# Rotary tables made first: positions with the constants, steps between the row tiles' scalings, sines stored ahead of the second half's norm

## The chip, the core and the metric

The kernel runs on one core of a Trainium2 chip. The metric is the device time of one execution in microseconds (us), as the median of several runs. TensorE (PE) does the matmuls, VectorE (DVE), ScalarE (ACT) and GpSimd (POOL) the elementwise work; SyncE (SP) issues nearly all DMAs. Each engine works through its own instructions in a fixed order and waits on semaphores.

## The reference

Two decoder layers on x of 1024 tokens by 1024, float32. The first layer mixes tokens by sliding-window attention with rotary embedding of the first quarter of each head (64 wide), the second by a gated recurrence; each is set between two RMS norms and added to x.

```python
def partial_rope(x, positions):          # half = 8 of 64
    inv_freq = ROPE_THETA ** (-(arange(8) * 2.0 / 16))
    ang = positions[..., None] * inv_freq
    cos, sin = cos(ang), sin(ang)        # per token and frequency
    r1 = x1 * cos - x2 * sin
    r2 = x2 * cos + x1 * sin
...
h = rmsnorm(x, pre_norm_w[0])
q, k, v, z = split(h @ w_in + b_in)
q, k = partial_rope(q), partial_rope(k)
o = softmax over a window of 128 keys (q k^T / 8, with a sink per head) @ v
x = x + rmsnorm((o * silu(z)) @ w_out + b_out, post_norm_w[0])
... (second layer: projections, chunked recurrence, projection)
```

## The kernel before

Matmuls are done in three products of split operands: a weight tile `wraw` (128 x 512, 256 KB) is loaded by SP, split into a rounded high part `whi` (POOL for the first 20 tiles, ACT later) and a remainder `wlo` (DVE; POOL for tiles 2 and 3). Four `wraw` buffers rotate, so tile i+4 is loaded only when tile i has been split. Activations are split the same way: a transposed block `pst` in PSUM becomes `acth` (ACT) and `actl` (DVE).

The start: the 1024 rows come in two halves of four row tiles of 128. `x_load(o0, 0)` loads the first half, ACT squares each row tile, POOL makes the inverse root `rstd`, DVE scales the row tile (`norm_rows`), PE transposes it (L237), and the first two projections (values, and a quarter of the queries, `q_unit(0, 1, 0)`) run on the first half of the tokens. The second half, `xh1`, goes the same way after it: four squares (L225), four `rstd`, four scalings, transposes. Then come `q_unit(0, 2, 0)`, `q_unit(0, 3, 0)`, `q_unit(0, 0, 0)` (the one whose result is rotated: `qf`, `qtB`, L355 to L361) and `k_unit` (keys, rotated: `kf`, `tK`, `KH`, `KL`). `kw` are the split weight tiles 10 and 11 of the keys. `vmid`, `VX` belong to the values.

The rotary tables: DVE makes the angles from `pos` in about 25 small steps on 128 x 64 or 128 x 256 elements (tiles `rt`, `a1r`), ACT takes the sines (`cs`, L302 and L307, after a table load), POOL negates one (L308), SP stores them to `csd` in DRAM and reads them back, broadcast to all partitions, as `cosT` (512 KB), two halves of `sinT` (256 KB each), and four small pieces into `cosK`. The DVE steps are issued a few at a time between other work: `at` gives how many at each place (`some()`).

Queries go to DRAM in pieces (`qd`, L367) and come back transposed by head and block as `QS` (L497), which the first attention scores (`pss`, L514) read.

What sets the order: a scheduler orders the instructions of each engine by priority and by its own estimate of times. `tc.high_priority` and `hp()` raise the priority; with `v.on` DVE's instructions keep the order in which they are written; `tc.issue_after` puts an instruction behind another one. PSUM tiles rotate through two buffers per tag (`mm`, `t`, `s`, `o`), so that a transpose or a product also waits until the tile two before it on its tag has been read.

Of the kernel before, what the change touches and what calls it, by code (L numbers as in the profile page):

```python
# [89 lines left out]
def emit(tc, I, out):  # L90
    nc = tc.nc
    v = InOrder(tc, nc.vector)
    from contextlib import ExitStack
    top = ExitStack()
    with top:
# [13 lines left out]
        pos = const.tile([P, 64], I32, name="pos")  # L109
# [8 lines left out]
        def hp():  # L118

            return tc.high_priority(offset=HP)  # L120
# [10 lines left out]
        def fetch(end):  # L131
            while W["fetch"] < min(end, NS):
                f = W["fetch"]
                W["dmas"][f] = nc.sync.dma_start(wraw[f % NR], I["w"][f])
                W["fetch"] += 1

        def advance(end=NS):

            while W["split"] < end:
                i = W["split"]  # L140
                fetch(i + NR)
                if i in (W_K, W_K + 1):
                    W["place"][i] = W["keys"][i - W_K]
                elif W["free"]:
                    W["place"][i] = W["free"].pop(0)
                else:
                    return
                raw, (hi, lo) = wraw[i % NR], W["place"][i]
                with hp():
                    on_pool = i in (2, 3)  # L150
                    if i < 20:
                        nc.gpsimd.tensor_scalar(hi, raw, 1.0, 1.0, op0=ALU.mult, op1=ALU.mult)
                    else:
                        nc.scalar.activation(hi, raw, AF.Copy)  # L154
                    W["split_ins"][i] = (nc.gpsimd if on_pool else v).tensor_tensor(lo, raw, hi.bitcast(F32), op=ALU.subtract)  # L155
                W["split"] += 1
# [20 lines left out]
        def act_from_psum(k, half, ps, scale):  # L177
            hi, lo = act[k, half]
            ins = nc.scalar.activation(hi, ps, AF.Copy, scale=scale)
            W["actl"][k] = v.scalar_tensor_tensor(lo, ps, scale, hi.bitcast(F32), op0=ALU.mult, op1=ALU.subtract)  # L180
            return ins
# [51 lines left out]
        def transpose_half(hns, half, scol, then={}):  # L233
            for k in range(NK):
                pt = pp.tile([P, 512], F32, tag="tso"[k % 3], name="pst")
                for j in range(4):
                    nc.tensor.transpose(pt[:, j * P:(j + 1) * P], hns[j][:, k * P:(k + 1) * P], ident)  # L237
                ins = act_from_psum(k, half, pt, cst[:, scol + k:scol + k + 1])
                then.get(k, lambda: None)()
            return ins  # L240
# [13 lines left out]
        def x_load(xh, half):  # L254
            for j in range(4):
                t = half * 4 + j
                for cs in halves(t):
                    nc.sync.dma_start(xh[:, j, cs], I["x"][t * P:(t + 1) * P, cs])
# [14 lines left out]
        def rope_tables(sp, cosT, sinT, cosK, tK):  # L273

            ang, a2, acc = [sp.tile([P, 64], F32, name=f"rt{i}") for i in range(3)]
            t0, t1 = [sp.tile([P, 4, 64], F32, name=f"rt{i}") for i in (3, 4)]
            a1r = sp.tile([P, 64], F32R, name="a1r")
            a1 = a1r.bitcast(F32)
            c1, c2, c3 = _split12(1.0 / (2.0 * np.pi), 2)

            def neg_frac(x):

                t = t1 if x is t0 else t1[:, 0, :]
                return [lambda: v.tensor_scalar(t, x, MAGIC, None, op0=ALU.add),
                        lambda: v.scalar_tensor_tensor(x, t, MAGIC, x, op0=ALU.subtract, op1=ALU.subtract)]

            steps = [lambda: v.tensor_copy(ang, pos),
                     lambda: v.tensor_scalar(ang, ang, cst[:, C_INV:C_INV + 1], None, op0=ALU.mult),
                     lambda: v.tensor_copy(a1r, ang),
                     lambda: v.tensor_tensor(a2, ang, a1, op=ALU.subtract),  # L290
                     lambda: v.tensor_scalar(acc, ang, c3, None, op0=ALU.mult)]
            steps += [lambda i=i, a=a, c=c: v.tensor_scalar(t0[:, i, :], a, c, None, op0=ALU.mult)
                      for i, (a, c) in enumerate(((a1, c1), (a1, c2), (a2, c1), (a2, c2)))]
            steps += neg_frac(t0) + neg_frac(t0)
            steps += [lambda i=i: v.tensor_tensor(acc, acc, t0[:, i, :], op=ALU.add) for i in range(4)]
            steps += neg_frac(acc)

            def last():
                cs3 = sp.tile([P, 3, 64], F32, name="cs3")
                lim, t2 = 0.49999997, t0[:, 0, :]  # L300
                v.tensor_scalar(t2, acc, lim, -lim, op0=ALU.min, op1=ALU.max)
                nc.scalar.activation(cs3[:, 1, :], t2, AF.Sin, scale=-6.2831853)  # L302
                v.tensor_scalar(acc, acc, -1.0, 0.25, op0=ALU.mult, op1=ALU.add)
                for f in neg_frac(acc):
                    f()
                v.tensor_scalar(t2, acc, lim, -lim, op0=ALU.min, op1=ALU.max)
                nc.scalar.activation(cs3[:, 0, :], t2, AF.Sin, scale=-6.2831853)  # L307
                nc.gpsimd.tensor_scalar(cs3[:, 2, :], cs3[:, 1, :], -1.0, 1.0, op0=ALU.mult, op1=ALU.mult)  # L308

                nc.sync.dma_start(csd.rearrange("i j (c n) -> (j c) i n", n=64), cs3)  # L310
                nc.sync.dma_start(cosT, csd[0:1].to_broadcast([16, 8, T]))
                nc.sync.dma_start(sinT[:64], csd[2:3].to_broadcast([8, 8, T]))
                nc.sync.dma_start(sinT[64:], csd[1:2].to_broadcast([8, 8, T]))
                m32 = sp.tile([P, M_L], I32, name="m32")
                nc.sync.dma_start(m32, I["msk"][:, :M_L])
                with tc.issue_after(W["rstd"].ins):
                    nc.gpsimd.memset(cosK, 1.0)
                    nc.gpsimd.memset(tK, 0.0)
                    nc.gpsimd.tensor_copy(msk, m32)
                for o in range(4):  # L320
                    nc.sync.dma_start(cosK[32 * o:32 * o + 8], csd[0])

            return steps + [last]

        def layer0():
# [3 lines left out]
            cosT = ka.tile([P, T], F32, tag="big0", name="cosT")  # L331
            sinT = ka.tile([P, T], F32, tag="big1", name="sinT")
# [38 lines left out]
            with pool("start", "right") as sp:  # L371
                W["keys"] = [tuple(kw.tile([P, 512], F32R, name=f"kw{i}{l}") for l in range(2)) for i in range(2)]
                kf = kw.tile([P, 512], F32, name="kf")
                tK = kw.tile([P, 512], F32, name="tK")
                cosK = kw.tile([P, T], F32, name="cosK")
                steps = rope_tables(sp, cosT, sinT, cosK, tK)
                at = iter([0, 3, 0, 4, 3, 3, 3])
                some = lambda: [steps.pop(0)() for _ in range(next(at))]
                with tc.high_priority(offset=1000):
                    v.on = True  # L380
                    hn0 = []
                    for j in range(4):
                        if j > 1:
                            some()
                        for cs in halves(j):
                            norm_rows(sp, o0[:, j, cs], o0[:, j, cs], rs0[j])
                        hn0.append(o0[:, j, :])
                    some()
                    advance(1)
                    last = transpose_half(hn0, 0, C_PRE, {2: lambda: advance(4)})  # L390
                xh1 = sp.tile([P, 4, D], F32, name="xh1")
                x_load(xh1, 1)
                hn1 = []
                with tc.high_priority(offset=1000):
                    for j in range(4):
                        with tc.issue_after(last.ins):
                            r = row_rstd(sp, xh1[:, j, :])
                        hn1.append(norm_rows(sp, xh1[:, j, :], xh1[:, j, :], r))
                        some()
                v.on = False  # L400
                with tc.issue_after(W["rstd"].ins):
                    advance()
                with hp():
                    while steps:
                        steps.pop(0)()
                nc.gpsimd.tensor_scalar(hbias, cst[:, C_BIN:C_BIN + 18], 0.5, 1.0, op0=ALU.mult, op1=ALU.mult)

                def k_unit(half):
# [55 lines left out]
            with pool("att", "right") as ap:  # L464
# [113 lines left out]
                at = [3, 5, 7, 7, 9, 11, 14, 14, 17, 19, 20, 23, 25, 27, 27]  # L578
# [362 lines left out]


        nc.scalar.dma_start(cst, I["cst"])
        x_load(o0, 0)
        nc.sync.dma_start(pos, I["pos"].unsqueeze(0).to_broadcast([8, 16, 64]))
        ld = const.tile([P, 9], F32, name="ld")
        v.tensor_tensor(ld[:, :8], cst[:, C_LB:C_LB + 8], cst[:, C_LB + 8:C_LB + 16], op=ALU.subtract)
        v.tensor_reduce(ld[:, 8:], ld[:, :8], axis=AX.X, op=ALU.max)
# [96 lines left out]
```

## Time and profile before

| | |
|---|---|
| runs | 920.67 us median of 3 (918.2 to 920.74) |
| the profiled execution | 919.34 us, span 917.5 us, granted clock 0.995 |
| PE busy | 891.1 us (97%) |
| DVE, ACT, POOL busy | 551.2, 373.7, 342.1 us |
| DMA | 78.61 MB, mean 86 GB/s |

The profile comes from one execution; its times are counted from the first instruction of the span. A view of waits tells which engine sat idle before an instruction, until what; the chain follows the work that ended last back to what released it; a timeline gives start and duration of each group of instructions; a view of stretches gives, for a piece of the span, each engine's busy time (and number of instructions), TensorE's granted clock, the DMA engines' busy share and GB/s. In rows, `out<-in` are the program's tiles without buffer numbers.

### The profile page before, as it was taken

Reading aid. Unit: us, or ns where it says so; the run is one execution under the profiler, and the core shown is the slowest. Engines: PE = TensorE matmul, PEld = TensorE weight load, DVE = VectorE, ACT = ScalarE, POOL = GpSimd, SP = SyncE. Lnnn points to the kernel's source line nnn. Section 1 sums busy time; section 2 is a strip of 40 time slices with the busy share of each in tenths; the row PEclk is TensorE's granted clock in tenths of the full one; section 3 lists DMA queues with packets and bytes.
Section 4 is the critical chain, followed back from the end, with each engine's and each line's share of the span. In section 5 each row is a group of like instructions: output and inputs, shape, how many; then the busy total and the mean of one; then the engine's idle time right before and its main releaser. Section 6 shows DMA issues by size and latency. Waiting matters only on the chain.

```text
span 917.5 us, 14082 instructions
## 1 busy us (share of the span) xinstructions
PE 891.1 (97%) x5214; PEld 744.8 (81%) x5214; DVE 551.2 (60%) x911; ACT 373.7 (41%) x958; POOL 342.1 (37%) x506
## 2 busy tenths in 40 slices
PE   6989999999999999999999999999999999999996
PEld 4868888888887788878888888888888788888885
DVE  6858887777876535762278864246866924252243
ACT  6525667666656332542322331423334124242311
POOL 5504465667787202330054422115424433210011
PEclk9999999999999999999999999999999999999998
DMA  8455364512311223540311010121111003032053
GB/s 285 143 153 157 107 185 130 166 54 62 90 54 59 91 63 129 177 149 19 106 50 36 24 47 1 51 66 35 35 47 48 1 1 92 1 98 86 24 183 119
DMA packets 53255, 78.61 MB, mean 86 GB/s; under 512 B 4760, under 2 KB 24984, under 8 KB 53176
## 3 DMA queue, kind: packets, MB, share of 16 engines
q1 hardware_dynamic: 53032, 77.51, 27.5%
q8 instruction: 43, 0.70, 0.3%
q14 instruction: 36, 0.29, 0.1%
q10 hardware_dynamic: 144, 0.10, 0.1%
HBM read 58.89 MB, written 16.88 MB: 83 GB/s over the span
## 4 chain that ended last, share of the span: by engine, by line
PE 72%; POOL 9%; DVE 7%; issue 5%; DMA 3%; ACT 2%; SPq 0%; POOLq 0%; ACTq 0%; DVEq 0%
PE psmm L189 59%; POOL rstd L217 2%; PE psk L834 1%; PE pso L847 1%; PE pss L514 1%; PE pss L515 1%; POOL ms L215 1%; PE pso L849 1%; PE pst L535 1%; POOL mY L546 1%; POOL mY L549 1%; DMA sinT<-csd 1%; PE pss L812 1%; PE pst L828 1%; PE pst L861 1%
## 5 line engine op out<-in xcount | busy, mean ns | idle before, releaser
L189 PE MATMUL psmm<-acth,whi 128*128 128x512 f32 x528 | 210.0, 398 | 1.6 <-DVE th L474 1.1
L189 PE MATMUL psmm<-acth,wlo 128*128 128x512 f32 x528 | 208.1, 394 | 0.2 <-POOL wlo L155 0.2
L189 PE MATMUL psmm<-actl,whi 128*128 128x512 f32 x528 | 208.2, 394 | 0.0
L189 PE MATMUL psmm<-whi,acth 128*128 128x512 f32 (+1 forms) x520 | 202.4, 391 | 1.0 <-DVE y L616 0.6
L189 PE MATMUL psmm<-wlo,acth 128*128 128x512 f32 (+1 forms) x520 | 201.2, 388 | 0.0
L189 PE MATMUL psmm<-whi,actl 128*128 128x512 f32 (+1 forms) x520 | 201.2, 388 | 0.0
L155 DVE TENSOR_TENSOR wlo<-wraw,whi 128x512 fp32r<-128x512 f32 x126 | 93.5, 754 | 95.6 <-ACT whi L154 91.2
L189 PEld LDWEIGHTS psmm<-acth,whi 128*128 128x128 f32 x528 | 99.6, 189 | 21.9 <-DVE th L474 2.2
L189 PEld LDWEIGHTS psmm<-acth,wlo 128*128 128x128 f32 x528 | 99.5, 189 | 19.9 <-POOL wlo L155 0.6
L189 PEld LDWEIGHTS psmm<-whi,acth 128*128 128x128 f32 x520 | 97.7, 188 | 21.2 <-DVE th L474 0.9
L189 PEld LDWEIGHTS psmm<-actl,whi 128*128 128x128 f32 x528 | 99.7, 189 | 18.4
L189 PEld LDWEIGHTS psmm<-whi,actl 128*128 128x128 f32 x520 | 97.7, 188 | 20.3 <-DVE actl L593 0.8
L189 PEld LDWEIGHTS psmm<-wlo,acth 128*128 128x128 f32 x520 | 97.8, 188 | 19.1
L154 ACT ACTIVATE whi<-wraw 128x512 fp32r<-128x512 f32 x112 | 69.9, 630 | 85.5 <-PE psmm L189 66.4
L529 ACT ACTIVATE sm<-sm,st 128x129 f32<-128x129 f32 x128 | 50.0, 392 | 52.0 <-DVE st L527 52.0
L698 POOL TENSOR_SCALAR gate<-gate,lbt 128x512 f32<-128x512 f32 x16 | 17.7, 1108 | 121.8 <-ACT gate L696 121.8
L908 DVE TENSOR_TENSOR y<-psmm,wpost 128x512 f32<-128x512 f32 (+1 forms) x17 | 11.2, 660 | 53.7 <-ACT jk L907 50.7
L217 POOL TENSOR_TENSOR rstd<-ms,nhalf 128x1 f32<-128x1 f32 (+1 forms) x48 | 41.8, 870 | 3.8
L546 POOL TENSOR_SCALAR_AFFINE_SELECT mY<-pT 64x256 fp32r<-64x256 f32 x56 | 29.3, 523 | 31.8 <-ACT pT L538 26.8
L907 ACT ACTIVATE jk<-psmm 128x512 f32<-128x512 f32 (+1 forms) x17 | 9.7, 571 | 66.9 <-PE psmm L189 66.9
L514 PE MATMUL pss<-KH,QS 128*128 128x256 f32 (+1 forms) x128 | 32.9, 284 | 3.8 <-DMA QS<-qd 3.8
L549 POOL TENSOR_SCALAR_AFFINE_SELECT mY<-pT 64x256 fp32r<-64x256 f32 x64 | 30.8, 481 | 6.0 <-ACT pT L538 1.4
(225 smaller groups left out, 1432.0 us busy)
## 6 DMA issues: line engine op xcount, KB each, us to landing
wraw<-in_w SPq DMA_DIRECT2D x132, 256.0 KB
QS<-qd SPq DMA_DIRECT2D x16, 512.0 KB
xr<-in_x SPq DMA_DIRECT2D x8, 512.0 KB
x1d<-xn SPq DMA_DIRECT2D x8, 512.0 KB
xr<-x1d SPq DMA_DIRECT2D x8, 512.0 KB
out_dram<-xn SPq DMA_DIRECT2D x16, 256.0 KB
xh<-in_x SPq DMA_DIRECT2D x4, 512.0 KB
qd<-qh SPq DMA_DIRECT2D x8, 256.0 KB
```

The lines of the kernel that those rows point to most:

```text
L154: nc.scalar.activation(hi, raw, AF.Copy)
L155: W["split_ins"][i] = (nc.gpsimd if on_pool else v).tensor_tensor(lo, raw, hi.bitcast(F32), op=ALU.subtract)
L189: nc.tensor.matmul(ps, a, b, start=(k == 0 and i == 0), stop=(k == NK - 1 and i == 2))
L215: keep(nc.gpsimd.tensor_scalar(m, ms, eps, 1.0, op0=ALU.add, op1=ALU.mult))
L217: W["rstd"] = keep(nc.gpsimd.tensor_tensor(r, m, nhalf[:, :width], op=ALU.pow))
L514: nc.tensor.matmul(ps[:, i, :nkk], q, KH[:, g, k0:k0 + nkk], start=True, stop=False)
L529: nc.scalar.activation(sm[:, h, :], sm[:, h, :], AF.Exp, bias=nm[:, h:h + 1], scale=0.125, accum_out=dn[:, h:h + 1])
L546: nc.gpsimd.affine_select(mY[r, :, :64], src[64:, :, :64].bitcast(F32), [[0, 4], [-1, 64]], ALU.is_gt, 0.0, base=0, channel_multiplier=1)
L549: nc.gpsimd.affine_select(mY[r, :, 64:], src[:64, :, 64:].bitcast(F32), [[0, 4], [1, 64]], ALU.is_ge, 0.0, base=0, channel_multiplier=-1)
L698: nc.gpsimd.tensor_scalar(dst, dst, ol, lb, op0=ALU.mult, op1=ALU.add)
L907: nc.scalar.activation(jk[:, c0:c1], ps, AF.Square, scale=D ** -0.5, accum_out=ss)
L908: v.tensor_tensor(y[:, c0:c1], ps, wpost[:, c * 512 + c0:c * 512 + c1], op=ALU.mult)
```

## The change

- The DMA that loads `pos` goes from SP's queue, behind the first half of x, to ACT's queue, right behind the constants.
- `at` is now 1, 2, 3, 4: ten of DVE's steps are written between the scalings of the first half's row tiles, ahead of the first weight split. All that is left of them, and the sines, their negation, the store to `csd` and the reads of `cosT` and `sinT`, is written directly behind the first half's transposes, ahead of the second half's load and norm, at raised priority. None are written between the second half's scalings any more.
- The masks and `cosK` go into a function of their own, `for_keys`, which is called where the last steps were made before.

```diff
                 nc.sync.dma_start(sinT[64:], csd[1:2].to_broadcast([8, 8, T]))
+
+            def for_keys():
                 m32 = sp.tile([P, M_L], I32, name="m32")
                 nc.sync.dma_start(m32, I["msk"][:, :M_L])
...
-            return steps + [last]
+            return steps + [last], for_keys
...
-                steps = rope_tables(sp, cosT, sinT, cosK, tK)
-                at = iter([0, 3, 0, 4, 3, 3, 3])
+                steps, for_keys = rope_tables(sp, cosT, sinT, cosK, tK)
+                at = iter([1, 2, 3, 4])
                 some = lambda: [steps.pop(0)() for _ in range(next(at))]
                 with tc.high_priority(offset=1000):
                     v.on = True
                     hn0 = []
                     for j in range(4):
-                        if j > 1:
-                            some()
+                        some()
                         for cs in halves(j):
                             norm_rows(sp, o0[:, j, cs], o0[:, j, cs], rs0[j])
                         hn0.append(o0[:, j, :])
-                    some()
                     advance(1)
                     last = transpose_half(hn0, 0, C_PRE, {2: lambda: advance(4)})
+                v.on = False
+                with hp():
+                    while steps:
+                        steps.pop(0)()
+                v.on = True
                 xh1 = sp.tile([P, 4, D], F32, name="xh1")
                 x_load(xh1, 1)
...
                         hn1.append(norm_rows(sp, xh1[:, j, :], xh1[:, j, :], r))
-                        some()
                 v.on = False
                 with tc.issue_after(W["rstd"].ins):
                     advance()
-                with hp():
-                    while steps:
-                        steps.pop(0)()
+                for_keys()
...
         nc.scalar.dma_start(cst, I["cst"])
+        nc.scalar.dma_start(pos, I["pos"].unsqueeze(0).to_broadcast([8, 16, 64]))
         x_load(o0, 0)
-        nc.sync.dma_start(pos, I["pos"].unsqueeze(0).to_broadcast([8, 16, 64]))
```

Where the scheduler puts the moved instructions is seen in the order of each engine. On SP's queue, from the weight tiles 6, 4, 7 and 5 on (the buffer's number is the tile's number modulo 4; the four buffers' next loads are tiles 8 to 11), before:

```order
L134 DMA wraw1_101<-in_w 128x512
L134 DMA wraw0_100<-in_w 128x512
L134 DMA wraw1_101<-in_w 128x512
L367 DMA qd_69<-qh_462 8x16x512
L134 DMA wraw2_102<-in_w 128x512
L134 DMA wraw3_103<-in_w 128x512
L367 DMA qd_69<-ql_463 8x16x512
```

```order
L367 DMA qd_69<-ql_550 8x8x512 x2
L310 DMA csd_71<-cs3_378 128x3x64
L311 DMA cosT_193<-csd_71 128x1x1024
L312 DMA sinT_194<-csd_71 64x1x1024
L313 DMA sinT_194<-csd_71 64x1x1024
```

The same place of the changed kernel, where the lines stand two further down:

```order
L134 DMA wraw1_101<-in_w 128x512
L310 DMA csd_71<-cs3_316 128x3x64
L311 DMA cosT_193<-csd_71 128x1x1024
L312 DMA sinT_194<-csd_71 64x1x1024
L313 DMA sinT_194<-csd_71 64x1x1024
L369 DMA qd_69<-qh_462 8x16x512
L134 DMA wraw0_100<-in_w 128x512
L134 DMA wraw1_101<-in_w 128x512
L134 DMA wraw2_102<-in_w 128x512
L369 DMA qd_69<-ql_463 8x16x512
L134 DMA wraw3_103<-in_w 128x512
```

The store of the sines and the three reads of the tables stood behind all weight tiles up to 15 and behind several stores of queries; now they stand directly behind tile 5, ahead of tiles 8 to 11 and of the first two stores of queries.

On DVE, between the last scaling of the first half and the first remainders of the activations, before:

```order
L87 TENSOR_SCALAR o0_136<-o0_136,rstd_176 128x512 x2
L87 TENSOR_TENSOR wlo0_90<-wraw0_100,whi0_80 128x512
L87 SCALAR_TENSOR_TENSOR actl0_0_105<-pst_235,cst_72,acth0_0_104 128x512
L87 SCALAR_TENSOR_TENSOR actl1_0_109<-pst_242,cst_72,acth1_0_108 128x512
L87 SCALAR_TENSOR_TENSOR actl2_0_113<-pst_249,cst_72,acth2_0_112 128x512
```

and now:

```order
L87 TENSOR_SCALAR o0_136<-o0_136,rstd_176 128x512 x2
L87 TENSOR_TENSOR wlo0_90<-wraw0_100,whi0_80 128x512
L285 SCALAR_TENSOR_TENSOR rt3_222<-rt4_223,rt3_222 128x256
L284 TENSOR_SCALAR rt4_223<-rt3_222 128x256
L285 SCALAR_TENSOR_TENSOR rt3_222<-rt4_223,rt3_222 128x256
L87 SCALAR_TENSOR_TENSOR actl0_0_105<-pst_242,cst_72,acth0_0_104 128x512
L295 TENSOR_TENSOR rt2_221<-rt2_221,rt3_222 128x64
L87 SCALAR_TENSOR_TENSOR actl1_0_109<-pst_249,cst_72,acth1_0_108 128x512
L295 TENSOR_TENSOR rt2_221<-rt2_221,rt3_222 128x64
L87 SCALAR_TENSOR_TENSOR actl2_0_113<-pst_256,cst_72,acth2_0_112 128x512
```

Three steps on 128 x 256 elements have moved in ahead of the first remainder, and single small steps between the next ones.

On DVE again, further on, at the splits of weight tiles 8 to 11 (`wlo8`, `wlo9`, `kw01`, `kw11`), what stands behind them in the changed kernel:

```order
L155 TENSOR_TENSOR wlo8_98<-wraw0_100,whi8_88 128x512
L155 TENSOR_TENSOR wlo9_99<-wraw1_101,whi9_89 128x512
L155 TENSOR_TENSOR kw01_213<-wraw2_102,kw00_212 128x512
L456 TENSOR_TENSOR VX_200<-pst_428,VX_200 128x8x64
L155 TENSOR_TENSOR kw11_215<-wraw3_103,kw10_214 128x512
L180 SCALAR_TENSOR_TENSOR actl0_1_107<-pst_468,cst_72,acth0_1_106 128x512
L180 SCALAR_TENSOR_TENSOR actl7_1_135<-pst_517,cst_72,acth7_1_134 128x512
L366 SCALAR_TENSOR_TENSOR ql_550<-psmm_524,cst_72,qh_549 128x512
```

Before, the remainders of the second half's blocks 1, 2, 4 and 5 stood between these splits, and all four splits stood ahead of `VX`; now they are ahead of the splits, and `VX` comes before the last split. `VX`, `actl0` and `ql_550` are the last readers of the PSUM tiles that PE's transposes of blocks 3 and 6 and the next product (`psmm_588`) write.

## The prediction

> **What bounds the kernel now.** First the page's head, then TensorE's waits in the first 200 us, then sums over short stretches, then the chain of waits that leads up to the long one.
>
> ```profile
> span 917.5 us, 14082 instructions
> ...
> PE 891.1 (97%) x5214; PEld 744.8 (81%) x5214; DVE 551.2 (60%) x911; ACT 373.7 (41%) x958; POOL 342.1 (37%) x506
> ```
>
> ```profile
> PE psl L950 <- DVE ld L948: 5.9, 1, 5.9
> PE pss L514 <- DMA QS<-qd: 3.8, 1, 3.8
> PE pst L237 <- DVE o L87: 2.5, 1, 2.5
> ```
>
> TensorE is the bound: 917.5 - 891.1 = 26.4 us idle in all, 8.4 of it in the first and third row's waits at the start. After the start one wait matters: 3.8 us at the first attention scores, for the queries QS read back from DRAM. The stretches (time, PE busy, ..., granted clock, DMA share, GB/s) show what it costs:
>
> ```profile
> 63.84:67.67 3.83, 0.00 (x1) 0.04 (x1) 3.67 (x6) 2.55 (x4) 0.00 (x0) 1.00 0.84 243
> ...
> 68.90:72.30 3.40, 3.40 (x11) 2.72 (x11) 3.37 (x6) 0.65 (x2) 0.89 (x2) 0.51 0.09 5
> ...
> 50.10:54.90 4.80, 4.80 (x23) 3.98 (x22) 0.68 (x1) 0.00 (x0) 0.00 (x0) 1.00 0.55 118
> ...
> 56.20:57.30 1.10, 1.10 (x7) 0.91 (x6) 0.97 (x2) 0.01 (x1) 0.00 (x0) 1.00 0.72 239
> ...
> 2.00:9.00 7.00, 0.58 (x2) 0.32 (x3) 1.65 (x6) 3.84 (x7) 1.82 (x4) 1.00 0.95 341
> ```
>
> PE is idle for 3.83 us; soon after it the clock is at 0.51 for 3.40 us, which loses 3.40 x 0.49 = 1.67. That is the most the change can win: 5.5 us. The chain (start, us, what) says why QS is late:
>
> ```profile
> 30.48 5.63 DMA wraw<-in_w
> ...
> 43.25 2.34 DMA csd<-cs
> ...
> 45.60 0.61 SPq L311
> ...
> 46.93 8.11 DMA sinT<-csd
> ...
> 55.07 0.70 DVE qtB L357
> ...
> 59.94 3.00 DMA qd<-ql
> ...
> 63.10 4.43 DMA QS<-qd
> ...
> 67.67 0.41 PE pss L514 x2
> ```
>
> The sines are stored only at 43.25, and the broadcast tables land at 46.93 + 8.11 = 55.04, or 9.44 us after the first of them (cosT) is issued at 45.60. The rotation of the queries waits for that.
>
> **The change, part by part.** Rows of ACT, DVE (its scalings as a group, with the idle time before them), POOL, SP and PE, otherwise by start:
>
> ```profile
> 18.42 0.69 ACT L179 ACTIVATE acth<-pst,cst 128x512 fp32r<-128x512 f32 x1 [0.81 <-PE pst L237]
> ...
> 23.52 0.18 ACT L225 ACTIVATION_READ_ACCUMULATOR jkx<-xh 128x1 f32 x1
> ...
> 32.56 1.28 ACT L302 ACT_TABLE_LOAD   x1
> ...
> 33.86 0.26 ACT L302 ACTIVATE cs<-rt 128x64 f32<-128x64 f32 x1
> ...
> 47.97 0.69 ACT L355 ACTIVATE qf<-psmm,cst 128x512 f32<-128x512 f32 x1 [1.60 <-PE psmm L189]
> ```
>
> ```profile
> L87 DVE TENSOR_SCALAR o<-o,rstd 128x1024 f32<-128x1024 f32 x3 | 2.3, 753 | 2.1 <-POOL rstd L217 1.1 <-ACT wraw L959 0.9
> ```
>
> ```profile
> 14.58 2.06 DVE L87 SCALAR_TENSOR_TENSOR actl<-pst,cst,acth 128x512 fp32r<-128x512 f32 x3
> ...
> 24.57 0.41 DVE L87 SCALAR_TENSOR_TENSOR rt<-rt,rt 128x256 f32<-128x256 f32 x1
> ...
> 25.01 0.29 DVE L87 TENSOR_SCALAR rt<-rt 128x256 f32<-128x256 f32 x1
> ...
> 26.82 0.83 DVE L87 SCALAR_TENSOR_TENSOR rt<-rt,rt 128x256 f32<-128x256 f32 x1
> ...
> 38.57 0.68 DVE L155 TENSOR_TENSOR kw<-wraw,kw 128x512 fp32r<-128x512 f32 x1
> ...
> 39.92 0.68 DVE L454 TENSOR_TENSOR VX<-pst,VX 128x512 fp32r<-128x512 f32 x1
> ...
> 40.53 0.74 DVE L180 SCALAR_TENSOR_TENSOR actl<-pst,cst,acth 128x512 fp32r<-128x512 f32 x1
> ```
>
> ```profile
> 3.40 0.79 SPq L945 DMA_DIRECT2D pos<-in_pos  x1
> ...
> 12.55 3.15 POOL L152 TENSOR_SCALAR whi<-wraw 128x512 fp32r<-128x512 f32 x4 [0.19 <-issue]
> ...
> 25.03 3.10 POOL L152 TENSOR_SCALAR whi<-wraw 128x512 fp32r<-128x512 f32 x4
> ...
> 36.19 1.25 POOL L152 TENSOR_SCALAR kw<-wraw 128x512 fp32r<-128x512 f32 x2 [3.69 <-DMA wraw<-in_w]
> ...
> 37.41 0.68 POOL L308 TENSOR_SCALAR cs<-cs 128x64 f32<-128x64 f32 x1
> ```
>
> ```profile
> 15.52 0.60 PE L237 MATMUL pst<-cst,o 128*128 128x128 f32 x4
> ...
> 17.21 0.50 PE L189 MATMUL psmm<-acth,wlo 128*128 128x512 f32 x1 [0.17 <-POOL wlo L155]
> ...
> 41.41 1.03 PE L237 MATMUL pst<-cst,xh 128*128 128x128 f32 x8
> ...
> 42.20 0.47 PE L189 MATMUL psmm<-acth,whi 128*128 128x512 f32 x1
> ```
>
> 1. *Positions on ACT's queue.* The issue, 0.79 us, moves from SP to ACT. ACT then waits for x anyway, so it costs nothing; without that cover it would be 0.79. The 32 KB now run among the row tiles: 0.1 us at 341 GB/s. SP reaches the first weight tiles 0.79 earlier, and nothing waits for those.
>
> 2. *Steps between the row tiles' scalings.* Ten small steps stand there now, three of them did before. DVE idles 2.1 us before the three scalings, and the seven new steps take at most 7 x 0.29 = 2.0 (25.01, a larger one): nothing. Without that cover they would add up to 2.0 to the next term.
>
> 3. *Steps that now stand ahead of the first remainders (actl).* Three 128x256 steps come between the first weight remainder and the first actl. They take 0.41 + 0.29 + 0.41 = 1.1 us beside an idle POOL and 0.83 + 0.29 + 0.83 = 1.95 beside a splitting one; POOL splits from 12.55 for 3.15 us, so I take 1.6. The four transposes of 15.52 start 0.25 after the first actl (14.58 + 0.69), so now at about 17.1. PE's work from there to the product of 17.21 is at most 17.21 - 0.17 - 15.52 = 1.5 us; I take 1.3, as matmuls overlap, and it comes at 18.4. **PE's start is later by 1.2 us** (bounds 0.7 and 1.6). What is left of the steps is under 0.3 us at a time between actl's that PE doesn't yet need.
>
> 4. *Sines ahead of the second half's norm.* In ACT's order the sines stand behind the four squares of that norm, which follow on the last acth and so on PE's transposes (18.42), and the POOL negation stands between the fourth mean and its root. The squares end at 23.70 + 1.2 = 24.9, the table load takes 1.28, the sine 0.26, the negation 0.68: the store csd goes at 27.2, not 43.25. The fourth root and the next weight splits on POOL are held up by some 2.9 us (25.03 to about 28), and PE comes to those weights only at 30: hidden, and if that cover were gone it would cost what is missing. SP stands still for csd's 2.34 us; cosT is issued at 29.5, and the last table lands 9.44 later, at **39.0 instead of 55.04**.
>
> 5. *What is queued behind the tables.* On SP's queue weight tiles 8 to 11 and two query stores stood ahead of csd; now they stand behind the two sine transfers. While those run (50.10 to 54.90) the DMA share is 0.55 at 118 GB/s: about half of the engines carry them, but a weight tile has rows on all. No row of before shows a load queued behind a table. The nearest, at 30.48, is a weight tile behind a query store, with 5.63 us to landing against 2.34 for csd. So I take it that the queue keeps its order on each engine. A store of 256 KB is put at 1.1 us (239 GB/s in the stretch at 56.20), a weight tile at 0.77 (341 GB/s). Tile 10 lands at 39.0 + 1.1 + 3 x 0.77 = 42.4, and after a second store tile 11 at 44.3.
>
> Who waits: DVE stands in order at the splits of tiles 8 to 10 and then of 11, and behind these are VX, actl and ql, which free the PSUM that PE's last transposes and the next product need. Tile 10: POOL 0.62, DVE 0.68, VX 0.68, so transposes at 44.4; PE is there at about 42.1 (41.41 + 1.2, less two products that now come behind). Tile 11: 44.3 + 0.62 + 0.68, then two actl and ql of about 0.66 each, 47.6. The product of 42.20 starts at 47.6: **5.4 us later**, the 1.2 of step 3 included. Bounds: 1.2, if the weight loads aren't held up, and 7.7, if each store costs 256 KB at 118 GB/s = 2.2 us.
>
> [...]
>
> 6. *The wait at the scores.* From the product of 42.20 to qf copied are 6.46 us (47.97 + 0.69); then 0.69 for the first half of qtB, and 67.67 - 55.07 = 12.60 to the scores: 19.8. PE needs 63.84 - 42.20 = 21.6 for its own work in between. **The wait goes (-3.83)**, with 1.9 us to spare; next late would be KL, which by the same rows is about as early.
>
> 7. *Clock.* The dip of 1.67 goes with the wait. The new waits at 42 to 47.6 are some 4 us with short bursts between them; a dip after them costs 0 to 1.67, and I take 1.2, since part of it would fall into the waits.
>
> Sum: +5.4 - 3.83 - 1.67 + 1.2 = **+1.1 us**. The profiled execution took 919.34 (span 917.5 and 1.8 around it), 1.33 below the median of 920.67; 920.4 by the one, 921.8 by the other, which I give.
>
> [...]
>
> **Rivals.**
> - *A trade (0.55):* one wait for another, as summed; own range 919.4 to 924.1.
> - *The loads aren't held up (0.17):* PE's stall at 42 doesn't come. For it: DMA share 0.55 while the tables run. Against it: 5.63 us of a tile behind a store. 1.2 - 3.83 - 1.67 = -4.3, so 916.4.
> - *The queue behind the tables is slower (0.22):* the two stores cost 2.2 us each, as tables do on their half of the engines. 5.4 + 2.2 = 7.6, sum +3.3 and 924.0. For it: 59.94, a store that took 3.00; against it: 239 GB/s at 56.20. It decides from about 1.9 us a store on (sum over +2.8).
> - *The wait at the scores stays (0.06):* the tables are earlier but the queries' way through DRAM takes 2 us more than in step 6. Each microsecond over 1.9 adds one; at 3 us more, +2.2 and 922.9.
>
> **How the numbers follow.** A measurement here tells about 0.3% (2.8 us) from no change. Forecast 921.8. Faster by more: the second case, with a margin of the first, 0.18. Slower by more: the third with the upper end of the first and fourth, 0.26. The rest 0.56. The range goes from the second case, 916.4, to 925.0, one above the third.
>
> **What would show it.** Right: csd issued near 27, a TensorE wait near 42 to 48 for DVE (VX, actl, ql) with POOL waiting for wraw, no wait for QS, and a clock dip near 45 to 52 in place of that near 70. Wrong in step 5: no wait at 42 and the span below 914. Wrong in step 3: PE's first long run not later than 17.2. Wrong in step 6: a wait for QS or KL at the scores.

## The result, and the profile after

The changed kernel takes 923.87 us (median of 10 runs, 922.17 to 925.29), the kernel before 919.84 (10 runs, 918.20 to 921.32): ratio 1.0043, 95% interval 1.0033 to 1.0054. It is slower by 4.0 us. A second series on another chip gave 1.0037 (1.0023 to 1.0050). The forecast was 921.8 in 916.4 to 925.0: one wait for another, with the likeliest sum too small. It gave 0.56 to a time within 2.8 us of the kernel before and 0.26 to a slower one; the slower one came.

The profiled execution took 925.0, near the top of the runs. Page head, TensorE's waits in the first 200 us, and four stretches (time, PE busy, ..., granted clock, DMA share, GB/s):

```profile
span 923.3 us, 14083 instructions
...
PE 894.5 (97%) x5214; PEld 746.8 (81%) x5214; DVE 553.0 (60%) x911; ACT 373.8 (40%) x958; POOL 341.6 (37%) x506
```

```profile
PE pst L237 <- DVE VX L456: 2.4, 1, 2.4
PE pst L237 <- DVE actl L87: 1.5, 1, 1.5
PE pst L237 <- DVE actl L180: 1.1, 1, 1.1
PE pso L559 <- POOL pT L556: 0.9, 2, 0.6
```

```profile
14.00:17.00 3.00, 1.07 (x3) 0.37 (x2) 2.93 (x6) 2.98 (x6) 3.00 (x5) 1.00 1.00 386
17.00:23.00 6.00, 5.90 (x23) 4.93 (x24) 6.00 (x13) 2.50 (x5) 1.78 (x3) 0.72 0.85 299
46.00:56.00 10.00, 8.51 (x28) 6.51 (x29) 5.87 (x15) 3.45 (x5) 2.28 (x6) 0.66 0.59 167
66.00:74.00 8.00, 8.00 (x38) 6.67 (x37) 7.05 (x10) 3.21 (x5) 0.72 (x1) 1.00 0.52 147
```

PE is idle for 923.3 - 894.5 = 28.8 us (26.4 before), and busy 3.4 us longer with the same matmuls: the clock (0.992 in the mean, 0.995 before). The wait for QS and the dip behind it are gone (66 to 74 at 1.00). In their place stand a wait of 1.5 us at the start with a dip behind it (0.72), and waits of 2.4 and 1.1 us at 44 to 48.6 with a longer dip (0.66). The chain (start, us, what) says why:

```profile
33.70 8.42 DMA wraw<-in_w
42.20 0.62 POOL whi L152
...
46.55 0.63 POOL kw L152
47.20 0.69 DVE kw L155
47.90 0.67 DVE actl L180
48.61 1.11 PE pst L237 x4
49.73 24.03 PE psmm L189 x95
73.76 0.17 PE pss L516 x2
```

Weight tile 8 is issued at 33.70 and lands 8.42 us later; the last key tile is split at 46.55. SP's rows show what stands ahead of them:

```profile
28.58 0.39 SPq L310 DMA_DIRECT2D csd<-cs  x1
30.88 0.64 SPq L311 DMA_DIRECT2D cosT<-csd  x1
...
32.30 0.58 SPq L313 DMA_DIRECT2D sinT<-csd  x1
32.98 0.61 SPq L369 DMA_DIRECT2D qd<-qh  x1
33.70 1.89 SPq L134 DMA_DIRECT2D wraw<-in_w  x3
```

How much later PE starts the same matmul, in the two profiled executions:

| place (time before) | later by | what came in between |
|---|---|---|
| 18.1 | 2.7 | wait for actl 1.2, dip 1.5 |
| 40.5 | 3.2 | |
| 42.2 (the product of step 5) | 7.8 | waits for VX and actl |
| 45.7 | 9.9 | dip |
| 67.7 (first scores) | 5.9 | before's wait for QS |
| 77 to 119 | 4.3 | before's dip |
| 128 | 5.7 | waits for POOL's pT |
| 909.0 (last matmul) | 5.9 | |

### The profile page after: what moved, and what is told of

It is laid out like the page before. It is cut to its first block, busy times and chain, and to the rows that moved or that the text cites. A ratio compares the mean times of both kernels' runs of the same rounds, so it can differ in the third digit from the quotient of the medians.

```text
span 923.3 us, 14083 instructions
## 1 busy us (share of the span) xinstructions
PE 894.5 (97%) x5214; PEld 746.8 (81%) x5214; DVE 553.0 (60%) x911; ACT 373.8 (40%) x958; POOL 341.6 (37%) x506
## 4 chain that ended last, share of the span: by engine, by line
PE 74%; POOL 8%; DVE 8%; issue 5%; ACT 2%; DMA 2%; SPq 0%; POOLq 0%; ACTq 0%; DVEq 0%
PE psmm L189 61%; POOL rstd L217 2%; PE psk L836 1%; PE pso L849 1%; PE pss L517 1%; PE pss L516 1%; PE pso L851 1%; PE pst L537 1%; POOL mY L548 1%; POOL mY L551 1%; POOL ms L215 1%; DMA wraw<-in_w 1%; PE pss L814 1%; PE pst L830 1%; PE pst L863 1%
## 5 line engine op out<-in xcount | busy, mean ns | idle before, releaser
L700 POOL TENSOR_SCALAR gate<-gate,lbt 128x512 f32<-128x512 f32 x16 | 17.7, 1108 | 121.9 <-ACT gate L698 121.9
L217 POOL TENSOR_TENSOR rstd<-ms,nhalf 128x1 f32<-128x1 f32 (+1 forms) x48 | 42.2, 880 | 3.7
L179 ACT ACTIVATE acth<-pst,cst 128x512 fp32r<-128x512 f32 x48 | 29.7, 691 | 18.0 <-PE pst L237 17.9
```

The lines of the kernel that those rows point to most:

```text
L217: W["rstd"] = keep(nc.gpsimd.tensor_tensor(r, m, nhalf[:, :width], op=ALU.pow))
L700: nc.gpsimd.tensor_scalar(dst, dst, ol, lb, op0=ALU.mult, op1=ALU.add)
```

## The experiments

Ratios are to the kernel before on the same chip. "Lateness" is that of the last matmul against the profile of before (909.0), "store to 8" and "store to 11" the time from the issue of csd to the split of weight tiles 8 and 11 on POOL; in the kernels before, e2, e5 and e6 tile 8 stands ahead of that store.

| kernel | ratio, 95% interval | lateness | wait for first actl | dip at 16 to 24 | store to 8 | store to 11 |
|---|---|---|---|---|---|---|
| changed | 1.0043 (1.0033 to 1.0054) | +5.9 | 1.5 | yes | 13.6 | 18.0 |
| a0, the same again | 1.0037 (1.0023 to 1.0050) | +4.2 | 1.5 | yes | 13.9 | 17.8 |
| b0, before again | | +2.0 | none | no | | |
| e5 start alone | 1.0000 (0.9989 to 1.0011) | -1.0 | 1.5 | no | | |
| e1 reads behind | 1.0045 (1.0032 to 1.0059) | +2.1 | 1.5 | yes | 6.9 | 15.1 |
| e4 reads in ACT's queue | 1.0010 (0.9999 to 1.0021) | +1.4 | 1.5 | yes | 12.9 | 17.7 |
| e7 sines in one read | 1.0035 (1.0024 to 1.0047) | +0.3 | 1.5 | no | 10.0 | 15.0 |
| e8 stores behind | 1.0053 (1.0039 to 1.0068) | +4.3 | 1.5 | yes | 12.8 | 15.6 |
| e2 both | 0.9998 (0.9988 to 1.0008) | -2.1 | none | no | | |
| e9 reads ahead | 1.0065 (1.0052 to 1.0078) | +3.8 | 0.5 | no | 13.8 | 16.6 |
| e6 steps spread | 0.9963 (0.9951 to 0.9975) | -4.7 | none | no | | |
| e10 positions alone | 1.0031 (1.0019 to 1.0044) | +0.9 | none | no | | |

In eight of the profiles (e1, e2, e4, e5, e7, e8, e9, e10) the end of the program, behind the last store, is 1.7 to 2.2 us longer than before; their ratios hold that too (last experiment). The lateness doesn't.

**The start alone (e5).** In the changed kernel, what is left after three more steps goes back between and behind the second half's scalings, and the sines' store behind tile 15:

```diff
-                    while steps:
-                        steps.pop(0)()
+                    for _ in range(3):
+                        steps.pop(0)()
...
+                        some()          # in the second half: 2, 2, 1, 1
...
+                with tc.issue_after(W["dmas"][15].ins):
                     csd, cosT, sinT
```

> The changed kernel's start alone: pos on ACT's queue, ten steps between the scalings and three ahead of the first actl; the other steps, the sines, their store and the reads stand late again, the store behind weight tile 15. Theory S: TensorE waits 1.2 to 1.6 us for the first actl, the clock falls to a half for about 3.4 us from 17 on, and TensorE is 2.5 to 3 us later at 30 than in the kernel before; the wait for QS stays but is shorter, since the tables are no later than before; span 917 to 920. Rival C (the dip at the start belonged to that one execution): 1.0 to 1.5 us later at 30, no dip before 25.

Its waits and the stretch at the start, and that stretch of a0:

```profile
PE pss L521 <- DMA QS<-qd: 1.5, 1, 1.5
PE pst L237 <- DVE actl L87: 1.5, 1, 1.5
```

```profile
17.00:23.00 6.00, 5.83 (x30) 4.90 (x31) 6.00 (x10) 3.93 (x7) 2.89 (x5) 1.00 0.81 290
```

```profile
17.00:23.00 6.00, 5.98 (x19) 4.96 (x20) 6.00 (x12) 2.10 (x3) 1.67 (x2) 0.52 0.77 264
```

PE is 1.25 us later, without a dip: on this point rival C holds. The same wait of 1.5 us was followed by a dip in five of seven profiles (2.7 to 4.3 us late then) and by none in two (1.1 and 1.25); six profiles without it (e9 with 0.5) had none. So the wait costs 1.2 and the clock 0 to 3, from one execution to the next. In the clock records of before and of the changed kernel the granted clock changes only at whole steps of 3.41 us from its first rise, and in all 13 profiles the twelve dips between 14 and 90 us are one such step (3.4 us) or two (6.8 us) long. In four of the five the fall came 0.3 to 0.6 us after the wait began (a0: wait from 15.50, fall at 15.96), in the changed kernel 1.5 us after, at 17.04. PE's work up to there doesn't decide it: from 14 to 17 it was 1.07 us in the changed kernel and the same 1.07 in e5, where the clock stayed at 1.00.

The 1.2 came out of the wait for QS (3.8 to 1.5): in e5 the start's loss costs nothing measurable. But e5 is not quite the start alone, since its store is issued at 39.30 (before: 43.25), which shortens the wait for QS too.

**Reads behind the weight tiles (e1), and in another queue (e4).** e1 issues the three reads behind tile 11; e4 leaves them early, on ACT's queue behind its first qh:

```diff
-                nc.sync.dma_start(cosT, ...)         # and both halves of sinT
+            def reads(): nc.sync.dma_start(cosT, ...)    # e4: nc.scalar
...
+                with tc.issue_after(W["dmas"][11].ins), hp():   # e4: behind qh
+                    reads()
```

> The changed kernel, but the three reads of the tables (cosT, both halves of sinT) stand on SP's queue behind weight tile 11 instead of ahead of tiles 8 to 11; the sines and their store stay early, the start is unchanged. Theory Q (the weight tiles were held up by the tables in the queue): tile 8 is split near 34 to 36 instead of 42.20, TensorE's waits at 46 to 49 and the clock dip behind them go, the start's loss of 2.7 us stays, no wait for QS; scores near 67 (73.8 in the changed kernel, 67.7 in the kernel before), span 916 to 918, ratio 0.998 to 1.001. Rival P (POOL and DVE were late for another reason, the norm of the second half or the late start): tile 8 is still split after 41, the wait stays, span 922 to 924.

> The changed kernel, but the three reads of the tables are issued by ACT, behind its first qh, so they stand in another queue than the weight tiles, and run at the same time as tiles 8 to 11. Theory Q (a load waits for what stands ahead of it in its own queue): tile 8 is split by 37, the waits at 46 to 49 are under 1 us together, span 917 to 919 with the start's loss of 2.7 us. Rival E (the engines are simply busy with the tables' packets, in whichever queue): tile 8 is split after 40, the waits stay at 2 us or more, span 920 to 924.

e1, SP and then POOL:

```profile
34.83 0.71 SPq L371 DMA_DIRECT2D qd<-qh  x1
35.64 0.99 SPq L134 DMA_DIRECT2D wraw<-in_w  x2
```

```profile
35.80 0.62 POOL L152 TENSOR_SCALAR whi<-wraw 128x512 fp32r<-128x512 f32 x1
40.92 0.62 POOL L152 TENSOR_SCALAR whi<-wraw 128x512 fp32r<-128x512 f32 x1 [4.50 <-DMA wraw<-in_w]
```

Tile 8 is split at 35.80 as theory Q said. But tile 9, right behind a query store, took 5.2 us to land, and PE still waited 1.6 us for VX. With the start's dip (3.6 us late by then) no gain over the kernel before was left: the last matmul comes 2.1 us later, 3.8 sooner than in the changed kernel, and the longer end hides that in the ratio. The expectation left out that a store holds up a tile by itself, though the prediction's row at 30.48 (5.63 us) had shown it.

e4, ACT's and SP's issues, then POOL:

```profile
31.84 0.58 ACTq L313 DMA_DIRECT2D cosT<-csd  x1
32.47 1.07 ACTq L314 DMA_DIRECT2D sinT<-csd  x1
33.51 0.34 SPq L134 DMA_DIRECT2D wraw<-in_w  x1
```

```profile
42.34 0.62 POOL L152 TENSOR_SCALAR whi<-wraw 128x512 fp32r<-128x512 f32 x1 [6.14 <-DMA wraw<-in_w]
```

In its own queue tile 8 had no table ahead of it, and landed nearly as late as in the changed kernel. The 0.7 us that it gained are no merit of the queue: the first query store stands behind tile 8 here, and e8 (below) gains 0.8 from that alone. Theory Q falls; rival E holds for the tile, though the wait for VX, 1.8 us, is a little under its 2: with the tables in the other queue the DMA share was 0.95 to 1.03 from 34 to 40 us. (The ratio is lower, 1.0010, since tile 8's delay was shorter by 0.7, no dip came behind it, and PE did not wait for pT at 124.)

**The two terms of the delay (e7, e8).** e7 reads the sines as the cosines are read; e8 puts the two query stores behind tile 11:

```diff
-                nc.sync.dma_start(sinT[:64], csd[2:3].to_broadcast([8, 8, T]))
-                nc.sync.dma_start(sinT[64:], csd[1:2].to_broadcast([8, 8, T]))
+                nc.sync.dma_start(sinT, csd[1:2].to_broadcast([16, 8, T]))
...
+                nc.gpsimd.tensor_scalar(sinT[:64], sinT[:64], -1.0, ...)   # behind tile 11's split
```

```diff
+                with tc.issue_after(W["dmas"][11].ins):      # q_unit(0, 1, 0) only
                     nc.sync.dma_start(qdh[...], q[...])
```

> The changed kernel, but the sines come in one read of the same shape as the cosines' (128 rows, 512 KB) in place of two halves of 64 rows; POOL negates the upper half behind its split of tile 11, and the store is a third smaller. Theory E (the weight tiles wait until the DMA engines have done the tables' packets, and a half of 64 rows runs on half of the engines): the tables end 2 to 3 us sooner, tile 8 is split at 39 to 40 (42.20 in the changed kernel), the last key tile at 43 to 44.5 (46.55), TensorE's waits for VX and actl fall from 3.5 us to 1 us or less; ratio to the kernel before 1.000 to 1.0025. Rival L (each transfer's latency counts, not the engines it runs on): tile 8 is split after 41, ratio 1.003 to 1.005.

> The changed kernel, but the two first query stores (qh and ql of the second quarter) stand behind weight tile 11 on SP's queue instead of ahead of tiles 8 and 11. It measures the stores' term: if a store holds the tiles up by 1.1 us as in the prediction, tile 8 is split near 41.2 and the last key tile near 44.4, and the ratio to the kernel before is 1.002 to 1.0035; if by 2.2 us, tile 8 near 40 to 41 and the last key tile near 42.2 to 43, ratio 1.000 to 1.0025; if the stores hold up nothing, 42.2 and 46.5, and 1.0045.

e7, the store's issue and POOL's first and last of the four splits:

```profile
27.24 0.39 SPq L309 DMA_DIRECT2D csd<-cs  x1
```

```profile
37.28 0.62 POOL L152 TENSOR_SCALAR whi<-wraw 128x512 fp32r<-128x512 f32 x1 [4.87 <-DMA wraw<-in_w]
...
42.23 0.62 POOL L152 TENSOR_SCALAR kw<-wraw 128x512 fp32r<-128x512 f32 x1 [1.12 <-DMA wraw<-in_w]
```

From the store to tile 8 it takes 10.0 us in place of 13.6: of these 3.6 us, 0.3 are the shorter store and 0.8 the first query store, which now stands behind tile 8 (e8). So the same bytes in one read of 128 rows cost some 2.5 us less here than in two of 64; from 34 to 36 us the DMA share is 1.02 at 224 GB/s in e7, 0.58 at 133 GB/s in the changed kernel. (The two forms also differ in how the source is repeated, 16 times against 8; no run separates the two.) VX is no longer waited for. Theory E holds for the tiles. The ratio lies above what I expected, where rival L had it: 1.7 us of it are the longer end, and this profile has no dip at all (clock 0.996), while the other runs had 0.992 to 0.995.

e8:

```profile
29.18 0.39 SPq L310 DMA_DIRECT2D csd<-cs  x1
```

```profile
41.97 1.83 POOL L152 TENSOR_SCALAR whi<-wraw 128x512 fp32r<-128x512 f32 x2 [6.02 <-DMA wraw<-in_w]
43.76 1.64 POOL L152 TENSOR_SCALAR kw<-wraw 128x512 fp32r<-128x512 f32 x2
```

Without the first store tile 8 comes 0.8 us sooner after csd, without both the last key tile 2.4 sooner (43.76 + 1.64 - 0.62 = 44.78, 15.6 after the store, against 18.0): 1.2 us a store, the prediction's 1.1, not 2.2. The gain is not in the ratio: the last matmul is 4.3 us late, as in a0 (4.2), 1.6 less than in the changed kernel's profile, but the end is 2.2 us longer.

**Steps spread, reads behind and ahead (e6, e9), and steps late in one piece (e2).** All three keep the positions on ACT's queue and the ten steps, and free the first actl:

```diff
-                at = iter([1, 2, 3, 4])
+                at = iter([1, 2, 3, 4, 3, 3, 3, 0])     # e6, e9: between the second half's scalings
...
+                with tc.issue_after(W["dmas"][11].ins):   # e6: csd and reads behind tile 11
+                with tc.issue_after(W["sinT"].ins):       # e9: tiles 8 to 11 behind the reads
...
+                with tc.issue_after(W["actl"][3].ins), hp():   # e2: the rest behind the fourth actl
                     while steps: steps.pop(0)()
```

> The changed kernel, but the steps of the tables that stood ahead of the first actl come behind the fourth actl; on SP's queue the store of the sines then stands behind tile 9 and the three reads behind tile 11. Theory Q with S (the start's loss is the three steps ahead of actl, with the clock dip that follows): TensorE's first long run starts near 15.7 as before, no dip near 17 to 20, no wait at 42 to 49, none for QS; scores near 64 to 65, 3 us earlier than in the kernel before; span 913.5 to 915, ratio 0.994 to 0.997 (not all of 5.5 us, since DVE and POOL bind the attention from there on and TensorE then waits 1 us or more for pT near 120 to 131). Rival N (sines ahead of the second half's norm cost by themselves: its roots, scalings and the next weight splits come 3 us late): waits for xh or whi appear near 28 to 32 and the span stays above 916.5.

> Positions on ACT's queue and ten steps between the first half's scalings as in the changed kernel; none of the steps ahead of the first actl, the other ones between the second half's scalings (3, 3, 3) and behind them, the store of the sines behind weight tile 11. Theory M (the loss lies in three places: DVE's steps ahead of actl, DVE's steps ahead of the second half's scalings, transfers ahead of tiles 8 to 11): TensorE waits neither near 17, nor near 29 for xh, nor at 42 to 49; the wait for QS falls under 1 us; the first scores come near 64 to 65 and TensorE is 3.5 to 4.5 us ahead of the kernel before at 100, of which 1.5 us go again in waits for pT at 115 to 130; ratio 0.995 to 0.9985. Rival D (DVE and POOL bind the attention so firmly that the gain goes entirely): ratio 0.999 or more.

> The kernel of e6_steps_spread with one thing put back: the store and the reads of the tables stand ahead of weight tiles 8 to 11 again (behind the first two query stores). Theory E (the tables' packets hold up the weight tiles): tile 8 is split 12 to 13.6 us after the store of the sines is issued, 43 to 46; TensorE waits 3 to 5 us near 42 to 47 for weights (whi, wlo) or for what stands behind their splits; ratio 3 to 5 us over e6, 0.9995 to 1.0025. Rival B (what cost the changed kernel its time was only the late start): ratio as e6, 0.995 to 0.9975.

e2, a wait of PE and the scalings of the second half on DVE:

```profile
PE pst L237 <- DVE xh L87: 1.9, 1, 1.9
```

```profile
26.53 4.67 DVE L87 TENSOR_SCALAR xh<-xh,rstd 128x1024 f32<-128x1024 f32 x4
```

The start and the tiles are as hoped, but DVE makes the steps up to 26.5, and only then the four scalings for which PE waits from 27: a loss of 2 us (rival N, though by DVE's order, not by POOL's). In the changed kernel, 2.7 us late, PE didn't see it. (The longer end is in the ratio of e2 too: its last matmul comes 2.1 us sooner than before.)

e6 has neither: it is the one version whose time beats both kernels, 0.9963 (0.9951 to 0.9975), 3.4 us below before, as theory M had it. The waits for pT that M expected didn't come. What is left is 1.0 us for QS:

```profile
PE pss L516 <- DMA QS<-qd: 1.0, 1, 1.0
```

e9 is e6 with the tables ahead again:

```profile
PE psmm L190 <- POOL whi L153: 5.6, 1, 5.6
```

```profile
33.42 0.39 SPq L311 DMA_DIRECT2D csd<-cs  x1
```

```profile
47.24 1.82 POOL L153 TENSOR_SCALAR whi<-wraw 128x512 fp32r<-128x512 f32 x2 [13.16 <-DMA wraw<-in_w]
```

Tile 8 is split 13.8 us after the store, and PE waits 5.6 us for it. From e6 to e9 the last matmul comes 8.5 us later: that is what the reads' place is worth there, where the store goes 4.8 us later than in the changed kernel (33.42 against 28.58). Rival B falls. I had expected 3 to 5 us; the dip behind the wait and the waits for pT (below) come on top.

**Positions alone, and the kernels again (e10, a0, b0).** e10 is the kernel before with this alone:

```diff
         nc.scalar.dma_start(cst, I["cst"])
+        nc.scalar.dma_start(pos, I["pos"].unsqueeze(0).to_broadcast([8, 16, 64]))
         x_load(o0, 0)
-        nc.sync.dma_start(pos, I["pos"].unsqueeze(0).to_broadcast([8, 16, 64]))
```

> The kernel before with only the load of the positions moved from SP's queue to ACT's. The prediction's first step: nothing, TensorE within 0.3 us of the kernel before at 60 and the wait for QS at 3.5 to 4 us; ratio 0.9985 to 1.0015. It also tells whether the 2 us that some of these kernels spend behind the last store depend on SP's number of instructions (one fewer here): then the time from the start of the last matmul to the end is near 10.4 us instead of 8.5, and the ratio 1.001 to 1.003.

> The changed kernel, unchanged, for a second profile and its clock. Theory S/C (the wait of 1.5 us for the first actl is always there; whether the clock falls to a half behind it differs from one execution to the next): the wait is 1.4 to 1.6 us, the dip at 17 to 20 may be there or not, the store of the sines is issued at 28.6 with it and near 27.2 without; tile 8 is split 13.6 us after that store; ratio 1.003 to 1.0055.

> The kernel before, unchanged, for a profile on the same chip as the next three. If the end of the program is what differs between chips, the time from the last matmul to the end of the span is near 7 us here as in the first four experiments (10.2 to 10.4 us from the start of the last matmul), not 8.5 as in the profile shown of before; the wait for QS is 3 to 4 us and a clock dip follows it. If the end depends on the kernel, it is 8.5.

PE runs 0.4 us ahead of before from 18 to 61, and waits as long for QS:

```profile
PE pss L514 <- DMA QS<-qd: 3.9, 1, 3.9
```

Yet the ratio is 1.0031. In this profile 1.2 us of that is a longer dip behind QS; the rest is the end. Here are the last stores, of before and of e10 (first issue's start, time to the last issue's end):

```profile
906.07 7.12 SPq L922 DMA_DIRECT2D out_dram<-xn  x4
```

```profile
906.94 7.19 SPq L922 DMA_DIRECT2D out_dram<-xn  x4
```

From there to the end are 917.5 - 913.2 = 4.3 us before and 920.4 - 914.1 = 6.3 in e10. The changed kernel has the short end too (4.4, and again in a0), so its result holds none of this. Nor did the chip make it: b0, beside three of the experiments, has 4.3. My guess was the number of SP's instructions, and the traces fit it: they count 509 in the five profiles with the short end (before, b0, changed, a0, e6) and 506 to 508 in the eight with the long one; e10 has 508, and its 10.6 us from the last matmul to the end (8.6 before) are what the guess expected. No run changes that number alone, so it is not shown to be the cause. a0 and b0 also show how far two executions of one kernel differ: by 1.7 and 2.0 us at the last matmul, mostly through longer or shorter dips.

## Why the prediction was right and wrong, step by step

1. *Positions: nothing.* Right for PE (e10).
2. *Ten steps between scalings: nothing.* Right: in e2 and e6 PE is on time at 18.
3. *Three steps ahead of actl: +1.2.* Right in size (1.25 in e5, 1.1 in e7). What was missing stands in step 7: the clock behind this wait, 1.5 us in the profiled execution.
4. *csd at 27.2, hidden.* The order was right: without a dip the store is issued at 27.24 (e7, which has no negation ahead of it), with it at 28.58. But the step counted only what POOL holds up. The longer delay is on DVE, where the last step of the tables waits for the first sine, with all four scalings of the second half behind it:

```profile
28.03 0.20 DVE L306 TENSOR_SCALAR rt<-rt 128x64 f32<-128x64 f32 x1 [3.06 <-ACT cs L302]
28.14 3.45 DVE L87 TENSOR_SCALAR xh<-xh,rstd 128x1024 f32<-128x1024 f32 x4
```

   PE waited for none of this, because it was late itself; with the start mended the cover was gone, and 1.9 us showed (e2).
5. *Behind the tables: +5.4.* The place of the delay was right, and the sizes nearly: from csd to the product of 42.20 the prediction has 47.6 - 27.2 = 20.4, the trace 50.0 - 28.6 = 21.4; store 1.2, not 1.1. The term itself came to 7.8, mostly because the dip at the start made csd 1.4 later. That the queue keeps its order on each engine was my estimate, from the row at 30.48, and no run shows it: with the reads in another queue tile 8 was split at 42.34, against 42.20 (e4).
6. *No wait for QS: -3.83.* Right (-4.0).
7. *Clock: -1.67 + 1.2.* This is the step that failed, three times. The start's dip was not counted (+1.5). The dip behind the new wait cost 2.1, not 1.2: it was two steps long (6.8 us). In a0 it was one step and began inside the waits, and PE was 8.0 us late behind it, not 9.9. And the old dip's 1.67 were gained at the scores and given back 50 us later:

```profile
124.36 0.50 PE L559 MATMUL pso<-pT,VX 128*128 128x512 f32 x1 [0.62 <-POOL pT L556]
...
130.72 0.50 PE L559 MATMUL pso<-pT,VX 128*128 128x512 f32 x1 [0.31 <-POOL pT L556]
```

Before, at half clock, PE came to this product 51.65 us after its first scores (67.67 to 119.32) and waited for nothing; at full clock it comes sooner, and the softmax on DVE, ACT and POOL, which starts with the scores, isn't done: POOL's pT for it is ready 50.6 us after the first scores before and 50.7 in the changed kernel. The two waits cost 1.45 us. a0, e1, e2, e5, e7, e8 and e9 show the same two waits. e4 and e6 don't: the same pT is ready 1.2 and 1.6 us sooner after the scores there, and why was not tried.

By its own steps: +1.1, with 2.4 more in step 5 (1.4 of it by the start's dip), 0.9 for the second dip and 1.45 given back, is the 5.9 of the profile. In the medians it is 4.0, since the dips differ from run to run: changed runs with a mean clock of 0.996 have spans of 920.4 to 920.9, those at 0.992 up to 923.3. The rival of slower stores (2.2 each) gave nearly the right time, 924.0, for a reason that e8 refutes: that is luck. Part of the nearness of 921.8 is luck too, since it adds +1.1 to 920.67, and the kernel before took 919.84 in the ten runs; the change was +4.0.

The clock: the row of before had a dip behind 3.83 us without work. The changed kernel had one behind the broken waits too: from 44 to 46 PE had 0.04 us of work, from 46 to 48 1.12, and the clock fell at 47.76. When it falls differs: at the start at 15.8 to 17.0 in five profiles, and in e5 and e7, with the same wait of 1.5 us, not at all. What decides that the traces don't show.

The queues: in the changed kernel tile 8, issued on one queue behind the reads, took 8.42 us to land. In e4 the reads are on ACT's queue, and from 31 to 43 us 288 packets of ACT's queue and 530 of SP's took 35.3% and 32.6% of the engines' time. Even so tile 8 is split only at 42.34. The traces don't tell which engine carried which packet, and so not in what order one engine took them.

## What to carry to other kernels

A table or a store that is put earlier in a queue isn't free, even where its own consumer waits for it: list what it now precedes (from e6 to e9 the reads' place was worth 8.5 us), and time it by the GB/s of a stretch in which it runs (118 for the sines' reads before, at a DMA share of 0.55); in e4 another queue did not get round it. Price a short wait with the clock that may fall near it, as a spread (here 0 to 3 us) and not as one number. When a wait before a long chain goes, ask whether PE or the chain sets the pace behind it: here 1.45 us of what was gained at the scores went again in waits for pT.

## What the runs showed of the hardware that I had not expected

- Behind a wait of 1.5 us among sparse matmuls the clock cost 0 to 3 us on top, up to twice the wait's length, differing from one execution to the next. The twelve dips between 14 and 90 us were 3.4 or 6.8 us long, one or two steps of 3.41 us.
- 512 KB to 128 partitions in one read held up the next tile some 2.5 us less than two reads of 64 partitions each (e7).
- A weight tile right behind a query store landed 5.2 us after its issue (e1) where one without took under 2.8 (issued 33.00, split 35.80); in a queue that is full anyway the same store adds 0.8 to 1.2 (e8).
- The time behind the last store was 4.3 to 4.4 us in five profiles and 6.1 to 6.5 in eight, and the two groups are parted by SP's number of instructions (509; 506 to 508). Of the difference between e10 and before 2.0 us (0.2%) lie there alone.
